# A decoder trunk step on one core: squares in two homes, a pair's sums postponed, a down tile in banks of its own, the samples' decay moved

## The chip, the cores and the metric

The kernel runs on one core of a Trainium2 chip. The metric is the device time of one execution in microseconds (us), as the median of several runs. The engines of the core that matter here are TensorE (PE in the profile; PEld is its loading of weights), VectorE (DVE), ScalarE (ACT), GpSimd (POOL), whose queue also issues DMA transfers that add to their destination, and SyncE (SP), whose queue issues most plain loads. Every engine works off its own instructions in a fixed order and waits at the first one whose inputs or whose destination aren't ready.

## The reference

512 prompt tokens and 8 sample tokens go through one trunk step: a half-step SwiGLU feed-forward net, a mixer, a second feed-forward net, a final norm.

```
h = h + 0.5 * _swiglu(_rms_norm(h, ffn1_norm[l]), ffn1_w_gate[l], ffn1_w_up[l], ffn1_w_down[l])
m, p, c, s = _hybrid_mixer(_rms_norm(h, mix_norm[l]), st_pool[l], st_conv[l], st_ssm[l], ...)
h = h + m
h = h + 0.5 * _swiglu(_rms_norm(h, ffn2_norm[l]), ffn2_w_gate[l], ffn2_w_up[l], ffn2_w_down[l])

def _rms_norm(x, g):
    return x * rsqrt(mean(x * x, axis=-1) + EPS) * g
def _swiglu(x, wg, wu, wd):
    return (silu(x @ wg) * (x @ wu)) @ wd
```

The model width is 1024, the hidden width 2816 (22 tiles of 128). The mixer projects once, then runs causal pooling over four windows, a causal convolution of four taps, and a state-space scan in chunks of 128 tokens with 16 heads; for each sample token the old state is multiplied by a decay `exp(dt * A)` with `A = -exp(a_log)` and a new term is added.

## The kernel before

All tokens lie side by side: the 520 columns (512 and 8) are two halves of 260, the 1024 features are 8 blocks `d` of 128 rows. A product in full precision is made of three matmuls (`mm3`, L132): every operand is split into a high part (a cast, L121 or L218 on ScalarE) and a low part (the rest, a subtraction on VectorE in L123 or L224), and high by high, high by low and low by high are summed in PSUM. Where a low part is made by `part_by_dma` (L217), ScalarE writes the negated high part and a POOL transfer adds the original from memory (L220).

The gate and up weights of one hidden tile `f`, and pairs of tiles of the first two chunks of the down product (`Down(c, d)`), are multiplied by a scheme that needs seven half-size products in place of eight: sums of weight blocks (`s1`, `s2` in `Ffn.sums`, L371, made on VectorE by L391 to L393 or partly by DMA) are split as well (`shi`, `slo`, suffixes c and d), and the activations have seven combinations each (`xth`, `xtl`; for the hidden activations `gs`). `product(f, p)` (L426) issues 12 matmuls. Product 4 uses the quarter (`qhi`, `qlo`, L409). The banks are `A` (two), `BE` (two double ones) and the tag `ps` (two), eight banks in all. Results leave them by copies `ac` (L451) and in `gates` and `close`. `LOW_ON_DVE` (L36) lists the pairs (f, u) whose low part is made on VectorE instead of by DMA.

The loads of weights go through `raw`, two buffers of a pair of 512 KB blocks each; a buffer is loaded anew when all its readers are done.

The opening (L655 to L697) loads the input, multiplies hidden tiles 0 and 1 in plain 32-bit matmuls (`plain`, banks P), sums the squares of the eight blocks `d` (`squares`, L168: a square on ScalarE into a home, an addition into `acc` on VectorE; the home of block d is half `d % 4 % 2` of one cell `sqs`), takes the root (L185, on ScalarE, which loads a table for it) and the reciprocal (L186), and makes the activations' combinations. `keep` (L288) copies the plain results out of PSUM; `plain_out` (L340) gates them, and for each odd `f` `keep_g` (L315) makes the sums of the pair (f-1, f) and their high and low parts: six instructions on VectorE and three on ScalarE (L330 to L338). The pair lies in `gq`, of which there is one buffer.

`stream` (L489) runs tiles 2 to 21 with the eight pairs `Down(0, d)` and `Down(1, d)` behind tiles 8 and 16. The last chunk of the down product (six hidden tiles) is plain `mm3` (`down`, L547): output block `d` gets a double bank `BE`, two buffers in turn, and `done(d)` evacuates it with L566. `after1` then prepares the mixer's input.

The mixer runs by an order written out by hand, `CONV_PLAN` and `GATE_PLAN` (L41, L44): b and x are projections with convolution, d the step sizes, p, c and m the pooling, A and B the two halves of a scan step, X and y the samples' parts, z, G, H, o, g, h the gating and output. `d1` calls `token_acs` and `sample_decay` (L1034), which has two SP transfers that spread the step sizes over rows (`sdt`), an Exp of `a_log`, a product on VectorE (L1041) and another Exp.

What is written is not the final order. A planner takes all instructions in program order as priority, `high_priority` raises some, `queued(...)` (L92) puts a block's instructions behind given ones on the same engine, `keep_in_program_order` fixes some among themselves, and the order on each engine comes out of a simulated timeline.

Of the kernel before, what the change touches and what calls it, by code (L numbers as in the profile page):

```python
# [10 lines left out]
F32 = mybir.dt.float32  # L11
# [6 lines left out]
P = 128  # L18
# [16 lines left out]
CHUNKS = (8, 8, 6)  # L35
LOW_ON_DVE = ((2, 0), (KF - 1, 1))  # L36
NG = 9
# [3 lines left out]
CONV_PLAN = (  # L41
    "b0 b1 d0 b2 b3 x0 x1 v0 d1 x2 x3 d2 X0 p0 y0 c0 A0 p1 x4 m0 x5 B0 c1 p2 m1 A1 x6 c2 A2 B1 x7 X1 m2 A3"
)
# [20 lines left out]
def tile_trunk_step(ctx: ExitStack, tc: tile.TileContext, ins: dict, outs: dict):  # L64
# [178 lines left out]
    class Ffn:  # L243
# [4 lines left out]
        def __init__(self, nx, i, wx, gp, direct):  # L248
            self.nx, self.i, self.wx, self.gp, self.direct = nx, i, wx, gp, direct
            self.states = None  # L250
            self.folded = CHUNKS[0] + CHUNKS[1] if i == 1 else 0
            self.held = {} if self.folded else {CHUNKS[0] + 1: None, CHUNKS[0] + CHUNKS[1] + 1: None}
            self.dram, self.gs, self.few = {}, {}, []
# [47 lines left out]
        def gate_home(self, f):  # L301
            if not self.folded:
                return self.wx.tile([P, 2, HB], F32, tag="tg", bufs=2, name=f"tg{self.i}_{f}")
            if f % 2 == 0:
                self.pair = self.wx.tile([P, 4, HB], F32, tag="gq", name=f"gq{self.i}_{f}")
            return self.pair[:, 1:3] if f % 2 else self.pair[:, 0::3]

# [7 lines left out]
        def keep_g(self, f, tg):  # L315
# [11 lines left out]
            if f % 2:  # L327
                gs = self.gs[f // 2] = self.new_gs(f"gs{f}")
                xg, xd = self.pair, self.nx[2].rearrange("p (b t) -> p b t", b=2)
                nc.vector.tensor_tensor(out=xd, in0=xg[:, 0::2], in1=xg[:, 3:4].to_broadcast([P, 2, HB]),  # L330
# [9 lines left out]
        def plain_out(self, f):  # L340
            tg = self.plain_kept[f, 0]
            scaled = nc.vector.tensor_tensor(out=tg, in0=tg, in1=self.nx[3].rearrange("p (b t) -> p b t", b=2),
                                             op=ALU.mult)
            nc.scalar.activation(out=tg, in_=tg, func=AF.Silu)
            up = self.plain_kept[f, 1] if (f, 1) in self.plain_kept else self.banks[f, 1][2][:, :, :HB]
            nc.vector.scalar_tensor_tensor(out=tg, in0=up, scalar=-1.0, in1=tg, op0=ALU.mult, op1=ALU.mult)
            self.keep_g(f, tg)
            return scaled.ins
# [60 lines left out]
        def quarter(self, f, src):  # L409
            n = f"{self.i}_{f}b"  # L410
            if self.folded:
                hi, lo = (self.wx.tile([P, 512], F32R, tag=t, name=f"{t}_{n}") for t in ("qhi", "qlo"))
                h, l = hi, lo
                if len(src.shape) == 3:
                    h, l = (t.rearrange("p (j c) -> p j c", j=4) for t in (hi, lo))
                if (f, 1) not in LOW_ON_DVE:
                    home = self.dram[f][1]
# [71 lines left out]
        def stream(self, before, last_chunk):  # L489
# [6 lines left out]
            for t in tiles:  # L496
# [4 lines left out]
                for p in (2, 5, 6, 3, 7) if t in (2, KF - 1) else (5, 6, 3, 7, 2):  # L501
                    self.product(t, p)
                self.gates(t)
                prev = t
            self.product(KF - 1, 4)
# [41 lines left out]
        def down(self, c, lo, hi, after):  # L547
# [3 lines left out]
            def part(d, ks):  # L551
                if d not in units:
                    with queued(*(self.closed if after is not None and d == 2 else ())):
                        units[d] = load_unit(ins[f"w{self.i}d"][d, :, lo * P : hi * P], n * P, f"{self.i}d{d}_{c}")
                    banks[d] = ps[0].tile([P, 2, 512], F32, tag="BE", bufs=2, name=f"dn{self.i}_{d}_{c}")
                wh, wl = units[d]
                for b in range(2):
                    for k in ks:
                        g = self.g[lo + k]
                        mm3(banks[d][:, b, :HB], ws(wh, k), ws(wl, k), g[:, 0, b], g[:, 1, b], k == 0, k == n - 1)  # L560

            def done(d):
                tag, nb = ("ac", 3) if self.folded else ("tg", 2)
                t = self.wx.tile([P, 2, HB], F32, tag=tag, bufs=nb, name=f"td{self.i}_{d}_{c}")
                hd = h[:, d].rearrange("p (b t) -> p b t", b=2)
                nc.vector.scalar_tensor_tensor(out=t, in0=banks[d][:, :, :HB], scalar=-0.5,  # L566
                                               in1=self.nx[3].rearrange("p (b t) -> p b t", b=2), op0=ALU.mult,
                                               op1=ALU.mult)
                if after is None:
# [79 lines left out]
    room = [*ffn1.cells("x2"), *ffn1.cells("x1"), *ffn1.cells("x0")]  # L649
    sqs = [t.bitcast(F32).rearrange("p (a b) t -> p a (b t)", a=2) for t in ffn1.cells("sq")[:1]][0]  # L650

# [10 lines left out]
    for j in range(KD // 2):  # L662
# [7 lines left out]
        with tc.high_priority() if j else nullcontext():  # L670
            for d in (j, j + KD // 2):
                squared = squares(nx1, wx1, d, "f1", sqs[:, d % 4 % 2])
        last = j == KD // 2 - 1
# [17 lines left out]
    for j in range(KD // 2):  # L691
        ffn1.plain(1, xg1[j], j, (1,))
    with tc.high_priority():
        ffn1.keep(1, (0,))
# [128 lines left out]
def mixer(tc, ins, outs, e):  # L823
# [210 lines left out]
    def sample_decay():  # L1034
        for j in range(2):
            nc.sync.dma_start(
                out=sdt[64 * j : 64 * j + 64],
                in_=scr_dt.rearrange("(q j) t -> j q t", j=2)[j].unsqueeze(0).to_broadcast([64, NX, NS]))
        aexp = mp.tile([P, NX], F32, tag="aexp", name="aexp")
        tc.keep_in_program_order(nc.scalar.activation(out=aexp, in_=vec[:, VEC["a_log"] : VEC["a_log"] + NX], func=AF.Exp))  # L1040
# [205 lines left out]
    def outs_a():  # L1246
# [9 lines left out]
        "v": lambda j: pool_weights(),  # L1256
        "y": lambda j: sample_bc(),
        "X": sample_x,
        "p": lambda j: pooled.append(pooling(j)),
# [114 lines left out]
```

## Time and profile before

| | us |
|---|---|
| median of 3 runs | 984.15 (982.54 to 985.11) |
| the profiled execution, its own time | 984.63 |
| its span, first to last instruction | 982.9 |
| TensorE busy | 964.4 |
| VectorE busy | 809.7 |
| ScalarE busy | 618.2 |
| GpSimd busy | 137.6 |
| first plain matmul of the opening starts | 4.43 |
| first matmul of tile 2 | 34.28 |
| mean granted TensorE clock | 0.995 |

A row of the timeline has the start, the duration, the engine, the line, the operation, what is written from what, the shapes, a count, and in brackets the idle time of the engine before it with what ended it. A row of waits has the engine and line, what it waited for, the total, the count and the longest. Waits of an engine that isn't the bound cost nothing by themselves; TensorE's do.

### The profile page before, as it was taken

The page shows a single profiled execution, that of the slowest core. Times are in us where ns is not written, and L with a number is a line of the kernel's source. Part 1 is how long each engine was busy: PE and PEld are TensorE (multiplying, and loading weights), DVE is VectorE, ACT ScalarE, POOL GpSimd, SP SyncE. Part 2 cuts the span into 40 slices and gives each one's busy share as a digit, 9 for nine tenths or more (in the row PEclk, how much of TensorE's full clock was granted, in tenths as well). Part 3 has the DMA queues.
Part 4 walks back from the last instruction along what each step waited for, and adds up shares of the span by engine and source line. Part 5 has one row for each costly group of instructions (what it writes and reads, how often), then busy time and mean ns, then how long its engine had stood idle before and what let it go on. Part 6 is the DMA issues. An engine that isn't in the chain of part 4 may idle for free.

```text
span 982.9 us, 19609 instructions
## 1 busy us (share of the span) xinstructions
PE 964.4 (98%) x7772; PEld 943.6 (96%) x7772; DVE 809.7 (82%) x1330; ACT 618.2 (63%) x1125; POOL 137.6 (14%) x215
## 2 busy tenths in 40 slices
PE   9899999999999999999999999999999999999996
PEld 8899999999999999999899999999999999999995
DVE  6888978888887688689978897999967899667886
ACT  6877767777676465585676674676643566514663
POOL 0111121111211000166241000100012000110010
PEclk9999999999999999999999999999999999999998
DMA  7767787787876333253244232523345433452232
GB/s 205 183 162 200 168 181 183 168 203 167 186 178 140 106 125 113 71 183 128 100 155 150 80 131 90 162 92 129 125 117 195 145 98 118 123 181 80 84 117 87
DMA packets 54828, 137.81 MB, mean 140 GB/s; under 512 B 7432, under 2 KB 19656, under 8 KB 54736
## 3 DMA queue, kind: packets, MB, share of 16 engines
q1 hardware_dynamic: 39840, 104.18, 31.7%
q0 software_dynamic: 14624, 32.25, 17.6%
q8 instruction: 61, 1.00, 0.4%
q14 instruction: 31, 0.25, 0.1%
q10 hardware_dynamic: 272, 0.13, 0.0%
HBM read 129.19 MB, written 7.34 MB: 139 GB/s over the span
## 4 chain that ended last, share of the span: by engine, by line
PE 77%; DVE 8%; DMA 5%; ACT 4%; issue 3%; POOL 1%; SPq 0%; DVEq 0%; ACTq 0%; POOLq 0%
PE A L137 8%; PE A L133 7%; PE A L136 7%; PE BE L137 6%; PE BE L133 5%; PE BE L136 5%; PE dn L137 4%; PE dn L133 4%; PE dn L136 4%; PE P L282 4%; PE wo L133 2%; PE wo L137 2%; PE wo L136 2%; DMA raw<-in_w1gu 2%; DVE A L952 1%
## 5 line engine op out<-in xcount | busy, mean ns | idle before, releaser
L137 PE MATMUL dn<-g,wlo_2d 128*128 128x260 f32 x256 | 72.4, 283 | 0.0
L133 PE MATMUL dn<-g,whi_2d 128*128 128x260 f32 x256 | 72.1, 282 | 0.0
L136 PE MATMUL dn<-g,whi_2d 128*128 128x260 f32 x256 | 72.1, 282 | 0.0
L391 DVE TENSOR_TENSOR s<-raw 128x1024 f32<-128x1024 f32 x39 | 47.6, 1220 | 14.2 <-DMA raw<-in_w1gu 11.7
L451 ACT COPY ac<-A 128x260 f32<-128x260 f32 x123 | 43.9, 372 | 17.7 <-PE A L137 16.9
L133 PEld LDWEIGHTS dn<-g,whi_2d 128*128 128x128 f32 x256 | 48.2, 188 | 0.0
L136 PEld LDWEIGHTS dn<-g,whi_2d 128*128 128x128 f32 x256 | 48.2, 188 | 0.0
L137 PEld LDWEIGHTS dn<-g,wlo_2d 128*128 128x128 f32 x256 | 48.1, 188 | 0.0
L1103 POOL DMA_DIRECT2D out_nss<-hs x16 | 8.7, 545 | 259.0 <-DVE hs L1101 258.9
L566 DVE SCALAR_TENSOR_TENSOR td<-dn,r_f 128x520 f32<-128x520 f32 x24 | 16.7, 698 | 32.4 <-PE dn L137 32.1
L121 ACT CAST whi_2d<-raw_2d 128x1024 fp32r<-128x1024 f32 (+1 forms) x18 | 18.5, 1027 | 36.9 <-PE dn L136 15.0
L133 PE MATMUL wo<-catg,whi_wo 128*128 128x260 f32 x128 | 37.1, 290 | 0.0
L133 PE MATMUL inz<-xh_mx,whi_inz 128*128 128x260 f32 x128 | 36.6, 286 | 0.0
L133 PE MATMUL inx<-xh_mx,whi_inx 128*128 128x260 f32 x128 | 36.4, 285 | 0.0
L137 PE MATMUL wo<-catg,wlo_wo 128*128 128x260 f32 x128 | 36.3, 283 | 0.0
L136 PE MATMUL inz<-xl_mx,whi_inz 128*128 128x260 f32 x128 | 36.2, 283 | 0.0
L137 PE MATMUL inz<-xh_mx,wlo_inz 128*128 128x260 f32 x128 | 36.2, 283 | 0.0
L136 PE MATMUL inx<-xl_mx,whi_inx 128*128 128x260 f32 x128 | 36.2, 282 | 0.0
L137 PE MATMUL inx<-xh_mx,wlo_inx 128*128 128x260 f32 x128 | 36.1, 282 | 0.0
L136 PE MATMUL wo<-catg,whi_wo 128*128 128x260 f32 x128 | 36.1, 282 | 0.0
L952 DVE SCALAR_TENSOR_TENSOR A<-U,h,A 128x544 f32<-128x544 f32 x36 | 28.3, 785 | 3.6 <-ACT A L950 3.2
L1099 ACT ACTIVATE so<-br,sxdt 128x128 f32<-128x128 f32 x64 | 20.4, 391 | 16.1 <-DMA br<-scr_bc 9.4
(2138 smaller groups left out, 4401.1 us busy)
## 6 DMA issues: line engine op xcount, KB each, us to landing
raw<-in_w2gu SPq DMA_DIRECT2D x44, 512.0 KB, 4.3
raw<-in_w1gu SPq DMA_DIRECT2D x41, 512.0 KB, 4.3
raw_2d<-in_w2d SPq DMA_DIRECT2D x16, 512.0 KB, 4.7
raw_wo<-in_w_out SPq DMA_DIRECT2D x12, 512.0 KB, 4.5
ab<-scr_acs SPq DMA_DIRECT2D x8, 512.0 KB, 4.0
h<-in_state_ssm SPq DMA_DIRECT2D x16, 256.0 KB, 3.1
raw_inz<-in_w_in SPq DMA_DIRECT2D x8, 512.0 KB, 4.1
hs<-in_state_ssm POOLq DMA_DIRECT2D x16, 256.0 KB, 3.7
```

Source lines behind the costliest of these rows:

```text
L121: cast = nc.scalar.copy(h, src)
L133: first = nc.tensor.matmul(ps, whi, xhi, start=start, stop=False, **kw)
L136: nc.tensor.matmul(ps, whi, xlo, start=False, stop=False, **kw)
L137: nc.tensor.matmul(ps, wlo, xhi, start=False, stop=stop, **kw)
L282: mm = nc.tensor.matmul(self.banks[f, u][b][:, :HB], ws(self.raw[f][:, u], j + 4 * q), xg[:, slot[q]], start=j == q == 0, stop=j == 3 and ...
L391: nc.vector.tensor_tensor(out=s1, in0=diag, in1=up0, op=ALU.add)
L451: nc.scalar.copy(keep, out[:, :HB])
L566: nc.vector.scalar_tensor_tensor(out=t, in0=banks[d][:, :, :HB], scalar=-0.5, in1=self.nx[3].rearrange("p (b t) -> p b t", b=2), op0=ALU.mult,
L952: nc.vector.scalar_tensor_tensor(out=A[:, :n], in0=U[:, j : j + n], scalar=w(j), in1=A[:, :n], op0=ALU.mult, op1=ALU.add)
L1099: nc.scalar.activation(out=o[:, q], in_=br, func=AF.Copy, scale=sxdt[:, j, b : b + 1]))
L1103: tc.keep_in_program_order(nc.gpsimd.dma_start(out=outs["nss"][:, b, 4 * g : 4 * g + 4], in_=hs))
```

## The change

1. Opening, squares: the home of block `d` is now `d // 4`, so blocks d and d+4 have one each. The tile `sq` that holds the homes gives a second cell to the pair of tiles 2 and 3 (`pairs[2]`), which had to use the one `gq` buffer.
2. Opening, copies: `keep(1, (0,))`, the copies of the gate result of tile 1, are queued behind the root on ScalarE.
3. Opening, sums: `plain_out(1)` no longer makes the sums of the pair (0, 1); `stream` makes them after the gates of tile 3, behind the latest low part on VectorE.
4. Tile 3: the low part of its first weights is made on VectorE (`LOW_ON_DVE` has (3, 0)).
5. Folded down tiles: the low part of the quarter is made on VectorE for all eight (`isinstance(f, int)` leaves them out of the DMA way).
6. Last down stage of the first net: output block d=2 gets two single banks `ps` in place of a `BE`, and is evacuated in two instructions of half the size.
7. Mixer: `sample_decay` keeps its transfers; the Exp, the product and the second Exp become `sample_exp`, stage `k0`, right behind `A0`.

```diff
-LOW_ON_DVE = ((2, 0), (KF - 1, 1))
+LOW_ON_DVE = ((2, 0), (3, 0), (KF - 1, 1))
...
-    "b0 b1 d0 b2 b3 x0 x1 v0 d1 x2 x3 d2 X0 p0 y0 c0 A0 p1 x4 m0 x5 B0 c1 p2 m1 A1 x6 c2 A2 B1 x7 X1 m2 A3"
+    "b0 b1 d0 b2 b3 x0 x1 v0 d1 x2 x3 d2 X0 p0 y0 c0 A0 k0 p1 x4 m0 x5 B0 c1 p2 m1 A1 x6 c2 A2 B1 x7 X1 m2 A3"
...
             if f % 2 == 0:
-                self.pair = self.wx.tile([P, 4, HB], F32, tag="gq", name=f"gq{self.i}_{f}")
-            return self.pair[:, 1:3] if f % 2 else self.pair[:, 0::3]
+                if f not in self.pairs:
+                    self.pairs[f] = self.wx.tile([P, 4, HB], F32, tag="gq", name=f"gq{self.i}_{f}")
+                return self.pairs[f][:, 0::3]
+            return self.pairs[f - 1][:, 1:3]
...
-            self.keep_g(f, tg)
+            if f and self.folded:
+                self.later.append(lambda: self.keep_g(f, tg))
+            else:
+                self.keep_g(f, tg)
...
-                if (f, 1) not in LOW_ON_DVE:
+                if isinstance(f, int) and (f, 1) not in LOW_ON_DVE:
...
                 self.gates(t)
+                if t == 3:
+                    with queued(*ends[1:]):
+                        self.later.pop()()
...
-                    banks[d] = ps[0].tile([P, 2, 512], F32, tag="BE", bufs=2, name=f"dn{self.i}_{d}_{c}")
+                    n1 = f"dn{self.i}_{d}_{c}"
+                    if after is not None and d == 2:
+                        banks[d] = [bank(f"{n1}{b}")[:, :HB] for b in range(2)]
+                    else:
+                        t = ps[0].tile([P, 2, 512], F32, tag="BE", bufs=2, name=n1)
+                        banks[d] = t[:, 0, :HB], t[:, 1, :HB], t[:, :, :HB]
...
-                nc.vector.scalar_tensor_tensor(out=t, in0=banks[d][:, :, :HB], scalar=-0.5,
-                                               in1=self.nx[3].rearrange("p (b t) -> p b t", b=2), op0=ALU.mult,
-                                               op1=ALU.mult)
+                r = self.nx[3].rearrange("p (b t) -> p b t", b=2)
+                for o, s, q in ((t, banks[d][2], r),) if len(banks[d]) == 3 else zip(
+                        (t[:, 0], t[:, 1]), banks[d], (r[:, 0], r[:, 1])):
+                    nc.vector.scalar_tensor_tensor(out=o, in0=s, scalar=-0.5, in1=q, op0=ALU.mult, op1=ALU.mult)
...
-    sqs = [t.bitcast(F32).rearrange("p (a b) t -> p a (b t)", a=2) for t in ffn1.cells("sq")[:1]][0]
+    spare = [t.bitcast(F32) for t in ffn1.cells("sq")]
+    sqs = spare.pop().rearrange("p (a b) t -> p a (b t)", a=2)
+    ffn1.pairs[2] = spare.pop()
...
-                squared = squares(nx1, wx1, d, "f1", sqs[:, d % 4 % 2])
+                squared = squares(nx1, wx1, d, "f1", sqs[:, d // 4])
...
-    with tc.high_priority():
+    with tc.high_priority(), queued(root):
         ffn1.keep(1, (0,))
...
+    def sample_exp():
         aexp = mp.tile([P, NX], F32, tag="aexp", name="aexp")
...
+        "k": lambda j: sample_exp(),
```

More of the change, by code (lines that the diff above doesn't have):

```diff
@@ L252, in __init__ @@
             self.held = {} if self.folded else {CHUNKS[0] + 1: None, CHUNKS[0] + CHUNKS[1] + 1: None}
-            self.dram, self.gs, self.few = {}, {}, []
+            self.dram, self.gs, self.pairs, self.few, self.later = {}, {}, {}, [], []
             self.w, self.A, self.BE, self.ac, self.g, self.tg, self.raw, self.banks, self.behind, self.plain_kept = (
@@ L328, in keep_g @@
                 gs = self.gs[f // 2] = self.new_gs(f"gs{f}")
-                xg, xd = self.pair, self.nx[2].rearrange("p (b t) -> p b t", b=2)
+                xg, xd = self.pairs[f - 1], self.nx[2].rearrange("p (b t) -> p b t", b=2)
                 nc.vector.tensor_tensor(out=xd, in0=xg[:, 0::2], in1=xg[:, 3:4].to_broadcast([P, 2, HB]),
@@ L559, in part @@
                         g = self.g[lo + k]
-                        mm3(banks[d][:, b, :HB], ws(wh, k), ws(wl, k), g[:, 0, b], g[:, 1, b], k == 0, k == n - 1)
+                        mm3(banks[d][b], ws(wh, k), ws(wl, k), g[:, 0, b], g[:, 1, b], k == 0, k == n - 1)
             def done(d):
```

## The prediction

> **What bounds the kernel now.** I read the busy times of the page first, then who waited for whom on TensorE, then the stretches around each wait.
>
> ```profile
> PE 964.4 (98%) x7772; PEld 943.6 (96%) x7772; DVE 809.7 (82%) x1330; ACT 618.2 (63%) x1125; POOL 137.6 (14%) x215
> ```
>
> TensorE works in 964.4 of 982.9 us, and the change removes no matmul. So it can win only where TensorE stands still or runs at a lower clock.
>
> ```profile
> PE A L137 <- DVE slo_2d L123: 1.2, 1, 1.2
> PE dn L133 <- DVE td L566: 1.1, 1, 1.1
> PE BE L133 <- ACT ac L451: 1.0, 2, 0.8
> PE px L1123 <- ACT X L954: 0.8, 1, 0.8
> PE A_Down(c=1, d=1)_2857 L133 <- ACT ac_Down(c=1, d=1)_1_2860 L451: 0.6, 1, 0.6
> PE pm L136 <- DVE catp L1008: 0.6, 1, 0.6
> PE A L137 <- DMA wlo_3a<-in_w1gu: 0.5, 1, 0.5
> PE P L282 <- ACT ac L295: 0.5, 1, 0.5
> PE A_Down(c=0, d=1)_1318 L137 <- DMA qlo_Down(c=0, d=1)b<-in_w1d: 0.4, 1, 0.4
> PE A L133 <- ACT shi_2d L121: 0.4, 1, 0.4
> ```
>
> Each row gives the total, the count and the longest wait. Four belong to the opening (slo_2d 1.2, shi_2d 0.4, wlo_3a 0.5, the copy ac 0.5: 2.6 us), one to the last down stage (td, 1.1), one to the folded down tiles (qlo_Down, 0.4), two to the mixer's convolutions (catp 0.6, X 0.8). The stretches (length, then busy time of PE, PEld, DVE, ACT, POOL, then the granted clock) show what else is lost:
>
> ```profile
> 41.00:45.00 4.00, 3.93 (x20) 3.94 (x21) 3.51 (x7) 2.98 (x6) 0.84 (x1) 0.59 0.90 267
> 48.00:60.00 12.00, 12.00 (x102) 12.00 (x101) 9.27 (x14) 7.85 (x14) 1.68 (x2) 1.00 0.60 149
> 123.00:140.00 17.00, 16.48 (x134) 15.94 (x133) 12.19 (x19) 10.55 (x16) 3.42 (x3) 1.00 0.89 197
> 330.00:340.00 10.00, 8.89 (x75) 8.72 (x74) 8.77 (x17) 5.81 (x12) 0.00 (x0) 1.00 0.24 79
> 440.00:480.00 40.00, 39.24 (x333) 36.24 (x332) 38.08 (x74) 25.63 (x50) 20.84 (x33) 1.00 0.35 124
> ```
>
> Right behind the opening's longest wait the clock is 0.59 for 4 us: 4.00 x 0.41 = 1.64 us that no wait shows. A wait of 1.1 us (330 to 340) and one of 0.8 (440 to 480) left it at 1.00.
>
> **Opening.** Three edits act on one chain: root, reciprocal, low parts, slo_2d.
>
> ```profile
> 20.40 0.64 ACT L175 ACTIVATE sq<-h 128x520 f32<-128x520 f32 x1 [1.95 <-DVE acc_f L176]
> 23.84 0.81 ACT L298 COPY gq<-P 128x260 f32<-128x260 f32 x2 [2.08 <-PE P L282]
> 24.08 1.04 PE L182 MATMUL psr_f<-acc_f,ones 128*128 128x260 f32 x4
> 25.97 0.84 ACT L185 ACTIVATE r_f<-psr_f,eps 128x260 f32<-128x260 f32 x2
> 37.37 0.68 DVE L393 TENSOR_TENSOR s<-s,raw 128x512 f32<-128x512 f32 x1
> 37.97 0.69 DVE L330 TENSOR_TENSOR acc_f<-gq 128x520 f32<-128x520 f32 x1
> 38.23 1.04 ACT L121 CAST shi_2d<-s 128x1024 fp32r<-128x1024 f32 x1
> 39.33 0.39 PE L133 MATMUL A<-xth_f,shi_2d 128*128 128x260 f32 x1 [0.39 <-ACT shi_2d L121]
> 39.80 1.22 DVE L123 TENSOR_TENSOR slo_2d<-s,shi_2d 128x1024 fp32r<-128x1024 f32 x1
> 44.88 0.70 DVE L224 TENSOR_TENSOR gs<-gq,gs 128x520 fp32r<-128x520 f32 x1 [0.46 <-ACT gs L223]
> 55.93 1.23 DVE L123 TENSOR_TENSOR slo_4c<-s,shi_4c 128x1024 fp32r<-128x1024 f32 x1 [2.70 <-ACT shi_4c L121]
> ```
>
> Squares: the last square waited 1.95 us on ScalarE because feature blocks d and d+4 shared a home. With a home each it need not. The matmul psr_f that takes the sum of squares shows no wait at 24.08, so alone this gives nothing; it can let psr_f go earlier (up to 1.95 us, 0 taken). Root: psr_f ended at 25.12, but ScalarE sat 2.08 us before the copies of L298 and then loaded the root's table, so the root began at 25.97. Put behind the root, the copies free 25.97 - 25.12 = 0.85 us for everything after it. The copy ac, for which TensorE waited 0.5, moves with it by more than that: 0.5 us gone.
>
> Postponed sums: between 37.97 and 39.80 VectorE does three of the first pair's six instructions, 1.83 us that stand in front of slo_2d. It ended at 39.80 + 1.22 = 41.02; less 1.83 and 0.85 it could end at 38.34. But shi_2d follows L393 and moves by 0.85 alone, to 37.38 through 38.42, so slo_2d runs 38.42 to 39.64. TensorE, free at 39.33 - 0.39 = 38.94, comes 0.5 sooner, at 38.44, needs slo_2d for its third matmul, by the 0.39 of the first shown at about 38.83, and still waits 0.81 of the 1.6 us: 0.8 won. As a wait of 0.8 left the clock at 1.00, I take the 1.64 us as won too.
>
> Low part of tile 3's first weights on VectorE: a subtraction of 1.22 us (the slo_2d row has its shape) replaces a ScalarE pass, a POOL transfer and its landing. It follows slo_2d in 39.64 to 40.86. TensorE first has 36 matmuls of tile 2 left, at 0.118 us each (12.00 us by x102 in 48 to 60) 4.2 us from 39.64, so it comes at 43.9: 0.5 us won. If the sums were still in front it would end 1.83 later, at 42.7, in time too.
>
> The sums land behind tile 3's gates instead, 1.83 plus three more of at most 0.70: at most 3.93 us. VectorE idles 12.00 - 9.27 = 2.73 us in 48 to 60, 2.70 of it before slo_4c; the rest, 1.2 us, would push tile 4's sums. Behind them stand slo_4c and slo_4d, for which TensorE would wait. I take 0, since TensorE waits for nothing in that stretch, and keep -1.2.
>
> Opening: 0.5 + 0.8 + 0.5 + 1.64 = 3.4 us (bounds: 1.64 and 1.2 less, 0.6; all waits and the clock, 4.2).
>
> The Trainium skill, "TensorE: Matmul & The Clock Gate", Part 1, says that the clock halves only after an idle window of about 3.4 us. Here the rows show 1.6 us of waits ahead of the 0.59, so by that rule alone these waits would not be its cause, and the sum would be 1.64 us less; the place of the 0.59, right behind them, speaks for the waits.
>
> **Last down stage.**
>
> ```profile
> 332.12 2.69 DVE L123 TENSOR_TENSOR wlo_1d<-raw_1d,whi_1d 128x768 fp32r<-128x768 f32 x3
> 334.74 1.30 DVE L566 SCALAR_TENSOR_TENSOR td<-dn,r_f 128x520 f32<-128x520 f32 x2
> 335.58 0.36 PE L133 MATMUL dn<-g,whi_1d 128*128 128x260 f32 x1 [1.11 <-DVE td L566]
> ```
>
> Tile d=2 waits 1.11 us for the bank of d=0, which td frees behind three low parts. Its own low part is the first of the three, ready a third of the way through them, at 333.0, so with banks of its own it starts at 335.58 - 1.11 = 334.47. The next in need of that bank, d=3, comes 36 matmuls or 4.2 us later, after td. Two evacuations of half size add at most 0.65 us on VectorE, under those 4.2. Won: 1.1 (bounds 0.5 and 1.1).
>
> **Quarters of the folded down tiles.**
>
> ```profile
> 123.62 7.46 DMA raw_Down(c=0, d=3)_1542<-in_w1d
> 246.18 5.19 DMA raw_Down(c=1, d=3)_3081<-in_w1d
> 251.45 1.05 ACT L218 CAST whi_Down(c=1, d=3)a<-raw_Down(c=1, d=3)_3081 128x1024 fp32r<-128x1024 f32 x1 [1.98 <-DMA raw_Down(c=1, d=3)_3081<-in_w1d]
> 254.43 0.37 ACT L451 COPY ac_Down(c=1, d=1)_1_2860<-A_Down(c=1, d=1)_2857 128x260 f32<-128x260 f32 x1
> q0 software_dynamic: 1990, 2.35, 52.7%
> ```
>
> Eight tiles each get a subtraction of 0.70 us (row at 44.88, nearly the same shape) on VectorE, 5.6 us in all, and lose a ScalarE pass and a POOL transfer. VectorE idles 17.00 - 12.19 = 4.81 us in 123 to 140, so 0.70 each fits. The wait for qlo_Down (0.4) goes. Against it: the raw block is free only after the subtraction, so the load of d+2 starts at least 0.70 later; the cast that waited 1.98 for it, and the copy ac queued behind that on ScalarE (254.43), for which TensorE waited 0.6, come later. For it: the accumulating transfers hold 52.7% of the DMA engines' time in 110 to 140 (last line), and the two loads, 7.46 and 5.19, differ by 2.3 us by what runs beside them. I set these two off: 0.4 won (bounds +1.0 with both waits gone, -5.2 if all eight loads come 0.70 later and TensorE with them).
>
> **Samples' decay.**
>
> ```profile
> 410.55 1.28 ACT L1042 ACT_TABLE_LOAD   x1
> 413.33 0.23 DVE L1041 TENSOR_TENSOR sdec<-sdt,aexp 128x64 f32<-128x64 f32 x1 [4.51 <-DMA sdt<-scr_dt]
> ```
>
> VectorE stands 4.51 us at the product of the decay, with the convolutions queued behind it, and ScalarE loads Exp between Silus. The two transfers of sdt stay where they are on SP's queue; the product and two Exps go behind the first scan step, where the data has long landed and Exp is in the table. TensorE then had work stored up, but from 440 to 480 VectorE is busy 38.08 of 40, and the waits on catp (0.6) and X (0.8) come out of that backlog. I take 1.0 of the 1.4 (bounds 0 and 1.4), as POOL's window sums stand in the same chain.
>
> **Sum.** 3.4 + 1.1 + 0.4 + 1.0 = 5.9. The order on the engines is computed anew, and the untouched waits on ac (1.0 in two) show what such an order leaves; I take off 0.6: 5.3. The profiled execution took 984.63 us (982.9 of span and 1.7 around it), 0.5 more than the median: 979.3 from the one, 978.9 from the other. Forecast 979.0.
>
> **Rivals.** (1) The postponed sums are too much for VectorE in 48 to 60: TensorE waits 1.2 us and the clock falls again, 1.64: 979.0 + 2.8 = 981.8. For it 3.93 against 2.73 idle; against it the lighter load before 48. (2) The slower side: the later release in the folded down tiles. If each of the eight loads waits 0.70 for the subtraction and 0.6 for half of a 1.22 instruction ahead of it, TensorE loses 8 x 1.3 = 10.4 us against 4.9 won elsewhere: 989.7. It decides from 8 x 0.98 us on, 4.9 + 2.95. For it: the copy at 254.43 had no slack. Against it: only one tile in eight waited so, and the accumulates leave the queue. (3) The 0.59 doesn't hang on the waits and stays: 980.6. The place of it speaks against; the Trainium skill's rule on idle windows (page and part above) would have it so. (4) The change doesn't do what it says in the opening: the computed order keeps slo_2d late, and 3.4 us fall away: 982.4.
>
> **Chances.** Forecast 0.50, (1) 0.14, (2) 0.13, (3) 0.13, (4) 0.10. About 0.3%, 2.95 us, is what can be told from no change: faster is below 981.2, slower above 987.1. Faster: nearly all of the forecast, most of (3) and a third of (1), 0.64; slower: (2), 0.13; the rest, 0.23, within. The range starts 3 us under the forecast, at 976.0 (all bounds for good: 4.2 + 1.1 + 1.0 + 1.4 = 7.7, and 984.15 - 7.7 = 976.4), and ends at 985.0, which takes in (1), (3) and (4) and leaves out (2).
>
> **What would show it.** Right: no wait of 1 us on TensorE before 60 us, a clock near 1.00 in 38 to 48, the root within 0.2 us of psr_f's end, no td wait near 330, no qlo_Down transfers, no 4 us wait of VectorE on sdt and no waits on catp and X. Wrong: new waits on slo_4c or slo_4d, TensorE waiting on ac or shi in every folded down tile, or a stretch of clock near 0.6 elsewhere.

## The result, and the profile after

The changed kernel takes 986.26 us, the median of 20 runs (984.31 to 988.37), against 984.25 us for the kernel before (20 runs, 981.47 to 986.92). The ratio is 1.0022, with a 95% interval of 1.0012 to 1.0032: 2 us slower, inside the 0.3% that was called no change, 7 us above the forecast and 1.3 us above its range. The execution profiled below has a span of 984.5 us. Its busy times, and TensorE's waits on the copies `ac` (total, count, longest):

```profile
PE 966.0 (98%) x7772; PEld 944.8 (96%) x7772; DVE 815.6 (83%) x1340; ACT 605.4 (61%) x1112; POOL 125.7 (13%) x206
...
PE A L133 <- ACT ac L456: 4.9, 3, 2.4
PE A_Down(c=1, d=1)_2849 L133 <- ACT ac_Down(c=1, d=1)_1_2852 L456: 1.2, 1, 1.2
...
PE A_Down(c=0, d=1)_1314 L133 <- ACT ac_Down(c=0, d=1)_1_1317 L456: 0.5, 1, 0.5
...
PE A_Down(c=1, d=2)_2973 L133 <- ACT ac_Down(c=1, d=2)_1_2976 L456: 0.3, 1, 0.3
```

Of the waits that the prediction listed, those on slo_2d, shi_2d, wlo_3a, td, catp, X and qlo_Down are gone. The copies `ac`, with 1.0 + 0.6 + 0.5 us before and one more of 0.2, now have 4.9 + 1.2 + 0.5 + 0.3 = 6.9. The stretches (length, busy time of PE, PEld, DVE, ACT, POOL, granted clock, DMA share, GB/s):

```profile
41.00:45.00 4.00, 3.82 (x30) 3.40 (x28) 3.46 (x6) 2.61 (x3) 0.00 (x0) 1.00 0.41 165
48.00:60.00 12.00, 11.90 (x99) 11.69 (x98) 11.42 (x18) 8.61 (x15) 1.68 (x2) 1.00 0.74 173
123.00:140.00 17.00, 16.47 (x136) 16.09 (x134) 13.36 (x20) 9.28 (x14) 0.84 (x1) 1.00 0.59 173
330.00:340.00 10.00, 10.00 (x86) 10.00 (x85) 4.60 (x7) 3.67 (x6) 0.00 (x0) 1.00 0.02 6
440.00:480.00 40.00, 40.00 (x342) 37.21 (x341) 38.20 (x76) 25.91 (x51) 22.09 (x34) 1.00 0.36 120
```

The last down stage (330 to 340) and the mixer (440 to 480) have no lost time left, and the opening has little (3.82 of 4 and 11.90 of 12 busy). In 123 to 140 the DMA engines are less busy than before (0.59 against 0.89), yet TensorE stands still as long (16.47 of 17 busy, 16.48 before).

To see where the time went, compare the start of the same product in both timelines. One of tile 4 shows the opening (before, then after):

```profile
59.08 0.28 PE L133 MATMUL BE<-xth_f,shi_4c 128*128 128x260 f32 x1
```
```profile
55.64 0.28 PE L133 MATMUL BE<-xth_f,shi_4c 128*128 128x260 f32 x1
```

So 3.44 us are won by then. About 0.8 of this lead is lost again by tile 7 (86.45 before, 83.80 after), ahead of any folded tile. In the folded tile c=0, d=2, 2.3 to 2.9 us of it are left, at product 4 of tile 9 nothing (162.70 before, 162.82 after). The lag is 0.6 us at tile 16 and 6.3 us at tile 18 (290.00 before, 296.31 after). By the convolutions at 537 us it is down to 1.7, with the waits on td, on catp, on X and on one copy `ac` (0.80 at 308.77) gone. The loss lies in the two stretches of folded down tiles and, the larger part of it, right behind each of them, at product 4 of tiles 9 and 17. How one tile comes late is seen in the rows of the timeline around c=0, d=1 (start, duration, engine, line):

```profile
120.23 0.62 ACT L223 CAST qhi_Down(c=0, d=1)b<-raw_Down(c=0, d=1)_1289 128x512 fp32r<-128x512 f32 x1 [0.18 <-PE A_Down(c=0, d=0)_1191 L136]
...
121.72 0.69 DVE L224 TENSOR_TENSOR qlo_Down(c=0, d=1)b<-raw_Down(c=0, d=1)_1289,qhi_Down(c=0, d=1)b 128x512 fp32r<-128x512 f32 x1
...
122.43 0.86 SPq L366 DMA_DIRECT2D raw_Down(c=0, d=3)_1537<-in_w1d  x2
...
127.21 1.05 ACT L218 CAST whi_Down(c=0, d=3)a<-raw_Down(c=0, d=3)_1537 128x1024 fp32r<-128x1024 f32 x1 [2.99 <-DMA raw_Down(c=0, d=3)_1537<-in_w1d]
128.17 1.04 ACT L121 CAST shi_Down(c=0, d=2)d<-s_Down(c=0, d=2)_1422 128x1024 fp32r<-128x1024 f32 x1
...
129.12 0.36 ACT L456 COPY ac_Down(c=0, d=1)_1_1317<-A_Down(c=0, d=1)_1314 128x260 f32<-128x260 f32 x1
...
129.53 0.39 PE L133 MATMUL A_Down(c=0, d=1)_1314<-gs,qhi_Down(c=0, d=1)b 128*128 128x260 f32 x1 [0.53 <-ACT ac_Down(c=0, d=1)_1_1317 L456]
...
131.18 0.62 ACT L223 CAST qhi_Down(c=0, d=2)b<-raw_Down(c=0, d=2)_1413 128x512 fp32r<-128x512 f32 x1 [0.20 <-PE A_Down(c=0, d=1)_1314 L136]
```

The reader is to see a ring. TensorE's product 4 of one tile frees the cell `qhi`; ScalarE casts the quarter (120.23 to 120.85); VectorE reaches the subtraction 0.87 us later and takes 0.69; only then is the raw block free, and SP issues the load of d=3 at 122.43. ScalarE, which works in its order, stands 2.99 us at the cast of that load. Behind it stand shi and the copy `ac`, for which TensorE's next product 4 waits, and that frees `qhi` again at 131.18. One turn is 10.95 us. The kernel without the quarters' edit (first experiment) shows the same ring without VectorE in it:

```profile
119.60 0.62 ACT L218 CAST qhi_Down(c=0, d=1)b<-raw_Down(c=0, d=1)_1290 128x512 fp32r<-128x512 f32 x1 [0.93 <-PE A_Down(c=0, d=0)_1192 L136]
120.24 0.86 SPq L366 DMA_DIRECT2D raw_Down(c=0, d=3)_1540<-in_w1d  x2
...
124.46 1.05 ACT L218 CAST whi_Down(c=0, d=3)a<-raw_Down(c=0, d=3)_1540 128x1024 fp32r<-128x1024 f32 x1 [0.92 <-DMA raw_Down(c=0, d=3)_1540<-in_w1d]
...
129.66 0.62 ACT L218 CAST qhi_Down(c=0, d=2)b<-raw_Down(c=0, d=2)_1415 128x512 fp32r<-128x512 f32 x1 [0.93 <-PE A_Down(c=0, d=1)_1316 L136]
```

The load goes out 0.02 us after the cast, and the turn is 10.06 us with TensorE waiting for nothing: there TensorE's own 84 matmuls (seven products of 12) set the pace, and ScalarE stands 0.93 us at the cast of the quarter until TensorE is done. With VectorE in the ring only 0.18 and 0.20 of that are left, and TensorE waits for the ring. A turn of 10.95 us alone doesn't show this, since the kernel before has one as long at the same tile (122.60 to 133.55), with TensorE waiting 0.41 us for the transfer of qlo; what shows it is who ends the waits. Over the eight tiles of the changed kernel the raw block is held 1.58 to 1.99 us from the end of the cast to the next load, and 0.02 or 0.03 us without edit 5.

The largest single loss is at tile 17, seen in the chain of waits (start, length, what). The load for tile 19 takes 6.75 us, and TensorE waits 2.39 us in the end:

```profile
279.48 0.65 ACT qhi_17b L218
280.12 0.02 issue
280.14 6.75 DMA raw<-in_w1gu
...
286.96 1.06 ACT whi_19a L218
...
289.01 1.03 ACT shi_18d L121
290.04 0.28 ACT ac L456
290.32 0.04 issue
290.36 0.39 PE A L133
```

VectorE holds nothing here: the quarter of tile 17 still goes by DMA, and the load is issued right behind ScalarE's cast. The cast comes late, and the load is slower as well: without edit 5 it is issued at 273.76 and the first of its two transfers lands after 3.41 us. There the accumulating transfer of wlo_18a (269.80, 5.14 us to landing) runs beside it for 1.2 us, here (278.82, 5.10 us) for 3.8. The load for tile 11, behind which TensorE waits 1.75 us at tile 9, shows the same, 6.64 us against 5.00. So part of the loss seems to come from a late load that falls on another transfer; this is read from the traces, and no run tests it by itself.

### The profile page after: what moved, and what is told of

It reads as the page before. It is cut to its first block, busy times and chain, and to the rows that moved or that the text cites. A ratio compares the mean times of both kernels' runs of the same rounds, so it can differ in the third digit from the quotient of the medians.

```text
span 984.5 us, 19586 instructions
## 1 busy us (share of the span) xinstructions
PE 966.0 (98%) x7772; PEld 944.8 (96%) x7772; DVE 815.6 (83%) x1340; ACT 605.4 (61%) x1112; POOL 125.7 (13%) x206
## 3 DMA queue, kind: packets, MB, share of 16 engines
q0 software_dynamic: 10256, 29.63, 15.7%
## 4 chain that ended last, share of the span: by engine, by line
PE 78%; DVE 7%; DMA 7%; ACT 4%; issue 3%; SPq 0%; DVEq 0%; ACTq 0%
PE A L133 7%; PE A L136 7%; PE A L137 7%; PE BE L137 5%; PE BE L136 5%; PE BE L133 5%; PE P L282 4%; PE dn L137 4%; PE dn L136 4%; PE dn L133 4%; DMA raw<-in_w1gu 4%; PE wo L133 2%; PE wo L137 2%; PE wo L136 2%; PE inx L133 2%
## 5 line engine op out<-in xcount | busy, mean ns | idle before, releaser
L582 DVE SCALAR_TENSOR_TENSOR td<-dn,r_f 128x520 f32<-128x520 f32 (+1 forms) x25 | 16.8, 675 | 32.5 <-PE dn L137 32.5
```

The costliest lines, as they stand in the source:

```text
L582: nc.vector.scalar_tensor_tensor(out=o, in0=s, scalar=-0.5, in1=q, op0=ALU.mult, op1=ALU.mult)
```

## The experiments

Every ratio is to runs of the kernel before on the same chip in the same batch, and "us" behind a ratio is that share of 984.25. Two theories stood at first. By the one (release), the later release of the raw block costs the time; by the other (supply), the loads come at a pace that DMA sets, and they eat any lead of TensorE whichever way the quarters go.

**Without the quarters' edit.** The changed kernel with edit 5 taken back:

```diff
-                if isinstance(f, int) and (f, 1) not in LOW_ON_DVE:
+                if (f, 1) not in LOW_ON_DVE:
```

> The changed kernel with edit 5 taken back: the quarters' low parts of the folded down tiles go by DMA again. Release theory (the subtraction on VectorE holds the raw block, so the loads behind it, ScalarE's cast of them and the copies ac queued behind that cast come late, and TensorE waits for ac): the waits on ac of 1.75 and 2.39 us near 163 and 290 go, the lead of 3.4 us of the opening is kept, and the time is about 984.2 - 5.5 = 978.7 (977.5 to 980). Supply theory (the loads come at a pace that DMA sets, and any lead of TensorE is eaten by them whichever way the quarters go): the lead is gone again by 170 us, only the last down stage and the mixer win, about 982 (981 to 983.5).

Measured: 977.09 us, ratio 0.9924 (0.9895 to 0.9953), 7.5 us faster than before. This beats both kernels, and lies 0.4 us below the range of the release theory. TensorE's waits on `ac` are back to a small size, and no folded down tile has one:

```profile
PE A L133 <- ACT ac L456: 1.1, 2, 0.7
...
PE BE L133 <- ACT ac L456: 0.5, 1, 0.5
```

Against the changed kernel's 1.0022 this is 0.0098, so edit 5 costs 9.6 us, give or take 3 by the intervals. The wait on qlo_Down, for whose end the prediction gave the quarters 0.4 us, is gone in this run too, without their edit.

**The quarters' edit alone.** The kernel before with edit 5:

```diff
-                if (f, 1) not in LOW_ON_DVE:
+                if isinstance(f, int) and (f, 1) not in LOW_ON_DVE:
```

> The kernel before with edit 5 alone. Release theory: slower by 4 to 8 us (988 to 992), with waits on ac behind both groups of folded down tiles. Supply theory: without a lead there is nothing to eat, and the eight accumulating transfers are gone: 983.2 to 985.2.

Measured: 994.22 us, ratio 1.0094 (1.0058 to 1.0130), 9.3 us slower, more than either theory said. With and without the other edits, edit 5 costs about the same, 9.6 and 9.3 us; as either figure is sure to some 3 us only, that they lie so close is partly luck.

**The opening alone.** The kernel before with edits 1 to 4.

```diff
-LOW_ON_DVE = ((2, 0), (KF - 1, 1))
+LOW_ON_DVE = ((2, 0), (3, 0), (KF - 1, 1))
...
```

> The kernel before with edits 1 to 4 alone (squares, copies behind the root, postponed sums, tile 3's low part). Release theory: the 3.4 us are kept to the end, 980.0 to 981.5. Supply theory: they are eaten between 60 and 170 us, 983.5 to 984.5.

Measured: 979.06 us, ratio 0.9950 (0.9929 to 0.9970), 4.9 us faster, a little past the forecast's 3.4 and with it inside the interval (3.0 to 7.0 us). In its trace the wait on qlo_Down at 132 us is gone as well.

**The quarter copied away first.** The changed kernel, where ScalarE copies the quarter into two cells of 128x256 and VectorE subtracts from the copy. So the raw block is free after ScalarE's passes, while VectorE's work stays and the transfers are gone:

```diff
-                    part(h, l, src)
+                    nc.scalar.copy(h, src)
+                    for q in range(2):
...
+                        nc.scalar.copy(held, src[:, js])
+                        nc.vector.tensor_tensor(out=l[:, js], in0=held, in1=h[:, js].bitcast(F32), op=ALU.subtract)
```

> The changed kernel, the subtraction still on VectorE, but from a copy of the quarter that ScalarE makes (two of 128x256), so that the raw block is free after ScalarE's passes, as before. Release theory: the loads start as early as with the DMA way, the waits on ac go, 978 to 980.5. If it isn't the release but VectorE's load of 5.6 us, or the missing transfers' order, that costs the time: near the changed kernel, 985 to 987.

Measured: 979.62 us, ratio 0.9942 (0.9921 to 0.9962). Of the 9.6 us, 7.9 are gone (1.0022 less 0.9942). The next load goes out 0.03 us after the cast of the quarter in all eight tiles. The release, not VectorE's subtraction as such, carries most of the loss.

**A column that holds the block.** The kernel without the quarters' edit, plus one VectorE instruction per folded tile on a single column (0.15 us):

```diff
                     part_by_dma(h, l, src, home)
+                    if not isinstance(f, int):
+                        seen = tmp.tile([P, 1], F32, tag="seen", name=f"seen_{n}")
+                        nc.vector.tensor_tensor(out=seen, in0=src[:, 3, P - 1 :], in1=h[:, 3, P - 1 :].bitcast(F32),
+                                                op=ALU.subtract)
```

> The changed kernel with the quarters' low parts back on ScalarE and the accumulating transfers, plus one VectorE subtraction of a single column per folded down tile that reads the raw block and the cast quarter. So the raw block is held until VectorE reaches that point of its queue, but VectorE gets next to no work and no transfer is removed. Release theory (the hold is what costs): the loads into raw start late as in the changed kernel, the casts whi of tiles 10, 11, 18, 19 wait for them and TensorE waits for ac; 982.5 to 987. Load theory (0.70 us of VectorE per tile, 5.6 us in all, is what costs): as without the edit, 976.5 to 978.5. The column is written to a cell that nothing reads.

Measured: 981.17 us, ratio 0.9958 (0.9940 to 0.9975), 3.3 us worse than without it. That is between the two expectations, and the intervals of the two ratios overlap (0.9953 and 0.9940), so this run speaks for the hold but doesn't settle it. The block came free 1.00 us after the cast at the tile shown above (cast to 121.29, load at 122.29), but over the eight tiles it is 0.22 to 1.93 us. The 12 runs spread from 977.64 to 986.64 us, and the profiled one is the slowest of them. How the cost grows with the length of the hold is therefore not shown.

**The whole hold with the transfers kept, and its control.** In place of the column the whole subtraction, in two pieces (0.75 us per tile) whose results nothing reads; in the control the pieces read the cast quarter twice, so VectorE does the same work at the same place of its queue and doesn't touch the raw block:

```diff
+                    for q in range(0 if isinstance(f, int) else 2):
...
-                        nc.vector.tensor_tensor(..., in0=src[:, js], in1=h[:, js].bitcast(F32), op=ALU.subtract)
+                        nc.vector.tensor_tensor(..., in0=h[:, js].bitcast(F32), in1=h[:, js].bitcast(F32), op=ALU.subtract)
```

> As the run with the one column, with the whole subtraction on VectorE (two pieces of 128x256, 0.75 us per tile) into cells that nothing reads; ScalarE's pass and the accumulating transfer of the quarter stay. So the raw block is held as long as in the changed kernel and VectorE has its load, while the transfers are not relieved. If hold and load are the whole cost and the relief of the transfers is worth nothing: 985 to 987. If the relief is worth something: over 987. If the missing accumulates themselves cost something (other landing times, the two loads that collide at tiles 9 and 17): under 984.

> As the run with the whole subtraction on VectorE and the transfers kept, but the two pieces read the cast quarter twice in place of the raw block and the cast quarter. VectorE has the same load (0.75 us per folded tile) at the same place of its queue, and the raw block is free after ScalarE's cast. Theory of the hold (the later release is what costs): 976.5 to 979 by the kernel before at 984.5, hardly more than with nothing on VectorE. Theory of the load: 984 to 990, most of what the held run lost. In between: both have a share. The pieces are written to cells that nothing reads.

Measured: with the hold 991.79 us, ratio 1.0063 (1.0038 to 1.0087); the control 978.56 us, ratio 0.9917 (0.9904 to 0.9931). One operand of one instruction makes 0.0146, 14.4 us. In both kernels the pieces stand between the same instructions on VectorE. VectorE's extra work costs nothing that can be measured (0.9917 against 0.9924). The timeline of the held kernel, then that of the control, at the tile shown above:

```profile
120.76 0.62 ACT L218 CAST qhi_Down(c=0, d=1)b<-raw_Down(c=0, d=1)_1294 128x512 fp32r<-128x512 f32 x1 [0.54 <-PE A_Down(c=0, d=0)_1196 L136]
...
122.53 0.88 SPq L366 DMA_DIRECT2D raw_Down(c=0, d=3)_1552<-in_w1d  x2
128.97 1.05 ACT L218 CAST whi_Down(c=0, d=3)a<-raw_Down(c=0, d=3)_1552 128x1024 fp32r<-128x1024 f32 x1 [4.29 <-DMA raw_Down(c=0, d=3)_1552<-in_w1d]
134.33 0.62 ACT L218 CAST qhi_Down(c=0, d=2)b<-raw_Down(c=0, d=2)_1423 128x512 fp32r<-128x512 f32 x1 [1.59 <-PE A_Down(c=0, d=1)_1324 L136]
```
```profile
120.91 0.62 ACT L218 CAST qhi_Down(c=0, d=1)b<-raw_Down(c=0, d=1)_1294 128x512 fp32r<-128x512 f32 x1 [0.93 <-PE A_Down(c=0, d=0)_1196 L136]
...
121.56 0.82 SPq L366 DMA_DIRECT2D raw_Down(c=0, d=3)_1552<-in_w1d  x2
...
125.80 1.05 ACT L218 CAST whi_Down(c=0, d=3)a<-raw_Down(c=0, d=3)_1552 128x1024 fp32r<-128x1024 f32 x1 [0.94 <-DMA raw_Down(c=0, d=3)_1552<-in_w1d]
130.98 0.62 ACT L218 CAST qhi_Down(c=0, d=2)b<-raw_Down(c=0, d=2)_1423 128x512 fp32r<-128x512 f32 x1 [0.93 <-PE A_Down(c=0, d=1)_1324 L136]
```

The control's ring turns in 10.07 us, the held one's in 13.57: the load goes out 1.77 us after the cast's start, against 0.65, and takes longer too (6.44 us from issue to the next cast, against 4.24). The tile shown is the one with the largest difference. The hold isn't as long as in the changed kernel, though the expectation says so: over the eight tiles it is 0.86 to 2.39 us, 1.34 in the mean, against 1.58 to 1.99, 1.73 in the mean. The shorter hold costs more here, 14.4 us against 9.6; the held kernel has the accumulating transfers and ScalarE's pass that the changed one lacks. The step from 1.0063 to 1.0022, 4.0 us, is an estimate of what it is worth to have them gone once the loads are late, and a rough one, since the holds and the batches differ too.

**One group of the two.** The changed kernel with the quarters on VectorE in the first group (c=0) alone:

```diff
-                if isinstance(f, int) and (f, 1) not in LOW_ON_DVE:
+                if (isinstance(f, int) or f.c) and (f, 1) not in LOW_ON_DVE:
```

> The changed kernel with the quarters' low parts on VectorE for the first folded group (c=0) alone; the second keeps ScalarE's pass and the transfer. If each folded group pays its own share: half of the loss, 980.5 to 982.5. If one late load shifts all that follows: nearer 977 or nearer 986.

Measured: 984.80 us, ratio 0.9990 (0.9975 to 1.0004). That is nearer the changed kernel than the one without the edit. By the ratios the first group takes 6.5 us of the 9.6, but these figures are loose by some 3 us, and 1.5 us of the profiled execution are lost near 757 us, with a wait of 1.15 us on wlo_2d in the second feed-forward net, where the edit has nothing (the opening alone and the decay alone have such a wait too, 1.32 and 1.41). In the changed kernel's own trace, set against the one without edit 5, it is the second group that costs more: it is 3.3 us behind by tile 11 and 10.4 by tile 19. So how the loss divides between the groups isn't settled.

**The quarter first in the queues.**

```diff
-                    part(h, l, src)
+                    with nullcontext() if isinstance(f, int) else tc.high_priority():
+                        part(h, l, src)
```

> The changed kernel with the cast and the subtraction of the folded down tiles' quarters raised to high priority, so that they come in front of other work queued on ScalarE and VectorE. Release theory: the raw block comes free about 1 us sooner than in the changed kernel and most of the loss goes: 978 to 982. If the subtraction as such costs, wherever it stands in the queue: 985 to 987. If work that is pushed back by it matters more than the raw block: over 987.

Measured: 985.24 us, ratio 1.0000 (0.9985 to 1.0015). Taken by its expectation this speaks for the subtraction as such. But in the two traces TensorE, VectorE, ScalarE and GpSimd have their instructions in the same order, so the priority changed nothing. The subtraction starts 0.85 us after the cast's end at the tile shown, against 0.87, and the block is held as long:

```profile
119.66 0.62 ACT L223 CAST qhi_Down(c=0, d=1)b<-raw_Down(c=0, d=1)_1289 128x512 fp32r<-128x512 f32 x1 [0.18 <-PE A_Down(c=0, d=0)_1191 L136]
...
121.13 0.69 DVE L224 TENSOR_TENSOR qlo_Down(c=0, d=1)b<-raw_Down(c=0, d=1)_1289,qhi_Down(c=0, d=1)b 128x512 fp32r<-128x512 f32 x1
...
121.84 0.89 SPq L366 DMA_DIRECT2D raw_Down(c=0, d=3)_1537<-in_w1d  x2
```

So this run tells nothing between the theories. It is a second measure of the changed kernel: 1.0000 against 1.0022 means that ratios from two batches can lie 2 us apart, as much as the changed kernel is slower than the one before.

**The casts behind the copies.** On ScalarE, the cast of a late block (d=2 and 3, tiles 9 to 11 and 17 to 19) goes behind the copy of product 7 of the tile two before; once in the changed kernel, once without the quarters' edit:

```diff
-            with queued(*first):
+            late = f in (9, 10, 11, 17, 18, 19) if isinstance(f, int) else f.d > 1
+            with queued(*first, *(self.sevens[-2:-1] if self.folded and late else ())):
```

> The changed kernel, all low parts of the quarters on VectorE, with one order changed: on ScalarE the cast of a weight block whose load is late (tiles d=2 and 3 of both folded groups, 9 to 11, 17 to 19) stands behind the copy ac of product 7 of the tile two before, for which TensorE's product 4 waits, and no longer in front of it. The raw block is held as long as before. Theory of the queue (late load, ScalarE standing at the cast, the copy behind it late, TensorE waiting): the waits on ac of 2.4, 1.75 and 1.2 us go and the time is 978 to 981. If it is the late weights themselves, or VectorE's load, that cost: the waits move to whi, wlo or shi and the time stays at 984 to 987.

> The changed kernel without the edit of the quarters and with the casts behind the copies as in the first run of this batch. Theory of the queue: the copies ac had waits of 1.1 us left with the quarters on ScalarE, so at most 1 us to win, 976 to 977.5. If the casts come too late for their own low parts now: 978 to 982, with waits on wlo.

Measured: 992.22 us, ratio 1.0069 (1.0055 to 1.0083), and 996.43 us, ratio 1.0105 (1.0091 to 1.0118). Both got slower, and slower than any of the expectations. The first one's waits:

```profile
PE A L137 <- DMA wlo_11a<-in_w1gu: 2.7, 1, 2.7
PE A L137 <- DMA wlo_19a<-in_w1gu: 2.7, 1, 2.7
PE A L137 <- DVE slo_10d L123: 1.2, 1, 1.2
PE A L137 <- DVE slo_18d L123: 1.2, 1, 1.2
PE A L133 <- ACT ac L458: 1.2, 4, 0.6
```

The waits on `ac` did shrink, from 6.9 to 1.2, as the queue theory has it. But the pass that prepares the low part went behind the cast and behind a gate's Silu, so wlo_11a and wlo_19a landed late. The second run shows that the new order costs 17.8 us (1.0105 less 0.9924) even where no load is late. It was no clean test of the link over ScalarE, and no remedy.

**The two small edits alone.** Edit 6 in the kernel before:

```diff
+                    if after is not None and d == 2:
+                        banks[d] = [bank(f"{n1}{b}")[:, :HB] for b in range(2)]
...
```

> The kernel before with the one edit in the last down stage: output block d=2 in two single banks, evacuated in two halves. Forecast's step: the wait of TensorE for td (1.1 us near 335) goes and nothing else changes, 1.1 us faster, 982.9 to 983.4. Rival: the double evacuation or the later block d=3 takes it back, 984.0 to 985.0, with a wait on td or dn in 335 to 350.

Edit 7 in the kernel before:

```diff
-d2 X0 p0 y0 c0 A0 p1
+d2 X0 p0 y0 c0 A0 k0 p1
...
+    def sample_exp():
```

> The kernel before with the one edit in the mixer: the Exp of a_log, the product and the second Exp of the samples' decay behind the first scan step. Forecast's step: VectorE no longer stands 4.5 us at the product, the waits on catp (0.6) and X (0.8) go, 1.0 us faster, 982.8 to 983.6. Rival: TensorE's work stored up covers the stall anyway and the waits come from the window sums, 984.0 to 985.0 with both waits still there.

Measured: 984.64 us, ratio 0.9995 (0.9978 to 1.0013), and 983.75 us, ratio 0.9986 (0.9969 to 1.0003). Neither total can be told from no change, but the stretches can. For the down stage, the kernel before and then the edit alone:

```profile
60.00:100.00 40.00, 40.00 (x335) 40.00 (x335) 33.96 (x51) 31.11 (x48) 6.28 (x8) 1.00 0.78 185
...
320.00:345.00 25.00, 23.89 (x199) 23.72 (x198) 17.23 (x33) 11.44 (x23) 0.00 (x0) 1.00 0.36 117
```
```profile
60.00:100.00 40.00, 38.56 (x319) 38.15 (x318) 32.99 (x50) 29.02 (x47) 5.88 (x7) 1.00 0.76 179
...
320.00:345.00 25.00, 25.00 (x210) 25.00 (x209) 17.99 (x37) 11.53 (x25) 0.00 (x0) 1.00 0.29 99
```

In its own place the edit wins 1.11 us of TensorE's time. It loses 1.44 between 60 and 100, with a wait of 1.27 us on a copy `ac` at 74.07, where the edit has nothing, in the execution that was profiled; whether the order or that execution is the reason was not tried. The decay's edit alone, in 440 to 480, where the kernel before has 39.24:

```profile
440.00:480.00 40.00, 40.00 (x346) 37.94 (x346) 38.29 (x74) 24.56 (x50) 20.82 (x30) 1.00 0.35 117
```

The wait on X (0.76) lay in this stretch, the one on catp (0.59, at 433.79) just ahead of it; both are gone in this run.

## Why the prediction was wrong

**The opening** came out as forecast in its sum and its mechanism: 3.44 us are won by tile 4, against 3.4. The parts differ, and that they add up so closely is partly luck: slo_2d, of whose wait 0.81 us were to stay, causes none any more, and one wait of 0.71 on a copy `ac` comes new. The squares were taken at 0, but psr_f starts 1.43 us sooner (22.65 against 24.08) and the root 2.68 sooner (23.29 against 25.97), where 0.85 was counted. The clock term held: 1.00 in 41 to 45, where it was 0.59. So rival (3), that the 0.59 doesn't hang on the waits, has fallen. Rival (1) has fallen too: with the postponed sums VectorE is busy 11.42 of 12 us between 48 and 60, and nothing waits for slo_4c or slo_4d. Rival (4) fell with the opening alone, 4.9 us faster.

**The last down stage** and **the decay** were right in their places: 1.11 us against 1.1, and both waits gone, 1.4, where 1.0 was taken. With the opening and the deduction of 0.6 for a new order, the sum without the quarters would have been 3.4 + 1.1 + 1.0 - 0.6 = 4.9. The run without them gave 7.5 us, with an interval of 4.6 to 10.3.

**The quarters** are the step that failed. It read "the load of d+2 starts at least 0.70 later", set this off against the relief of the transfers, and kept 0.4 us as won. The runs put a loss of 9.6 us in its place (9.3 in the kernel before). That the hold makes it, and not VectorE's work, is shown by the held kernel against its control, 14.4 us, and by the quarter copied away first. 14.4 less the estimate of 4.0 for the relief is 10.4, which agrees with 9.6 within the runs' scatter. Two things were mis-sized. The hold is not the subtraction's 0.70 us but 1.58 at c=0, d=1, and 1.73 in the mean of the eight tiles: 0.87 in VectorE's queue comes on top, as seen between 120.85 and 121.72. And it was compared with the wrong slack. "Only one tile in eight waited so" says that the other seven had some slack, not how much. The rows around c=0, d=1 give it: without the edit ScalarE stands 0.93 us at the cast of the quarter in each turn, less than the hold. There one turn is as long as TensorE's work, 10.06 us; with VectorE in the ring it is 10.95. Over the six turns of the two groups that makes 3.8 us (64.25 against 60.49). The rest is lost right behind the groups, at product 4 of tiles 9 and 17, where the prediction had no term, and by the clock.

What the step set against the hold was misread, too. The 52.7% are of all accumulating transfers between 110 and 140 us; of their 2.35 MB the quarters are three of 0.26 MB, a third. The 7.46 and 5.19 us are of different halves of a block: its two transfers took 4.53 and 7.46 us for c=0, d=3, and 5.19 and 6.10 for c=1, d=3. And the 0.4 us for the wait on qlo_Down were no gain of this edit beside the others: with the opening's edits that wait is gone without it.

**Rival (2)** had this mechanism, 8 x 1.3 = 10.4 us for it, and a chance of 0.13. That the later release costs the time is shown, and the price was near (9.6 net), but partly by luck: TensorE doesn't lose 1.3 us at each of eight tiles, it loses 3.8 over six turns and more behind them, at tiles whose quarters VectorE doesn't touch. The total came out 3.4 us better than its 989.7, because the price was 0.8 lower and the other edits won 7.5, not the 4.9 set beside it. What spoke against it, "the accumulates leave the queue", is true, but by the estimate of 4.0 us it is worth less than a third of what the hold costs. The link from the late load over ScalarE's queue to TensorE is read from the chain of waits, where all its members stand; the run that was to cut it changed too much to show it by itself.

## What to carry to other kernels

Before a low part, a copy or any other reader moves to another engine, ask which buffer that engine will now hold, and for how long: its queue counts, not only its instruction. Walk the ring that the buffer closes (free, load, first reader, what is queued behind that reader, free again) and compare its length with the pace of the bound engine; no wait in the profile doesn't mean much slack. The same instruction with another operand, which keeps the work and drops the hold, tells the cost of the one from that of the other. And follow a late load further than its own tile: here the larger part of the loss came one tile behind each group.

## What the runs showed of the hardware

The granted clock didn't follow the length of a wait simply. Behind TensorE's wait of 2.39 us it fell, and behind one of 1.75 us at tile 9 it stayed. In the held kernel a wait of 1.77 us, with one of 0.18 right behind it, was enough. The two stretches of the changed kernel, then the one of the held kernel:

```profile
162.80:166.80 4.00, 3.98 (x32) 3.97 (x33) 4.00 (x8) 2.76 (x6) 0.76 (x1) 1.00 0.82 165
...
290.40:294.40 4.00, 4.00 (x24) 4.00 (x25) 4.00 (x8) 2.69 (x6) 0.80 (x1) 0.67 0.86 167
```
```profile
132.00:136.00 4.00, 4.00 (x21) 4.00 (x22) 3.66 (x8) 1.99 (x5) 0.96 (x2) 0.59 0.46 72
```

The traces show more than that. In all fifteen, the changes of the clock lie on a grid of steps of 3.41 us, counted from the first change of that execution. Each fall before the last stage lasts one step at 0.50: 291.79 to 295.20 in the changed kernel, 131.88 to 135.29 in the held one, 41.75 to 45.16 in the kernel before. In the step ahead of it TensorE is busy 1.43, 1.55 and 1.79 us. The wait at tile 9 is cut in two by the grid at 162.08, and TensorE is busy 2.40 and 2.67 us in the two steps. So it matters where in the grid a wait falls. What share of a step decides isn't settled: in the run with the one column a step with 1.56 us busy (195.61 to 199.03) left the clock at 1.00.

The Trainium skill, "TensorE: Matmul & The Clock Gate", Part 1, has the clock halve after an idle window of about 3.4 us and calls the window free-running. The grid agrees with the second; the first doesn't hold here, as no wait is that long and the clock fell all the same.

Fewer transfers did not mean earlier loads. The changed kernel moves 2.62 MB less by accumulation (29.63 against 32.25; 2.1 of it are the quarters), the DMA share in 123 to 140 falls from 0.89 to 0.59, and the weights still come later, because the loads are issued later and some then take longer (6.75 us against 3.41 at tile 17).
